# Moving the transposed activations hT by 64 bytes in SBUF

## The chip, the core and the metric

The kernel runs on one core of a Trainium2 chip. The metric is the device time of one execution in microseconds (us); lower is better. Before the change it is 2646.88 us, the median of three runs (2641.51 to 2647.48).

## What is computed

A decoder trunk of two layers over 256 tokens of width 2048, in float32. Layer 0 mixes with retention (8 heads), layer 1 with block-sparse attention (16 heads; with 256 tokens and blocks of 256 it is causal attention with a relative-position bias). Each mixer is followed by a gated MLP with a causal depthwise convolution.

```python
for i in range(DEPTH):                       # DEPTH = 2
    hn = rms_norm(h, mix_norm[i])
    h = h + (retention_mixer(hn, ret_w_in[0], ret_gn[0], ret_w_out[0]) if i == 0
             else moba_mixer(hn, moba_w_qkv[0], moba_w_out[0], rel_bias))
    h = h + conv_ffn(rms_norm(h, ffn_norm[i]), ffn_w_up[i], ffn_conv_w[i],
                     ffn_conv_b[i], ffn_w_down[i])
return rms_norm(h, final_norm)
```

The weight matrices are 2048 x 12288 and 4096 x 2048 (retention), 2048 x 6144 and 2048 x 2048 (attention), and per MLP 2048 x 11264 and 5632 x 2048. They are read once, some 480 MB, and with 256 tokens every one of them is multiplied by a small activation matrix.

## The kernel before

**Products.** A float32 value is split into a high part in fp32r and the rest, also in fp32r; a product is the sum of high by high, high by low and low by high. The activations are kept transposed, 128 channels per partition chunk: `hT` is a tile of 128 partitions x 16 chunks x 512 elements, where the first 256 elements of a chunk are the high parts of the 256 tokens and the last 256 the low parts. `yT` (32 chunks, retention output), `oT` (16 chunks, attention output) and `actT` (44 chunks, MLP inner activations) have the same layout.

**The weight stream.** Weights come as units of 1 MB by DMA (`issue_dma`, three `raw` buffers). `issue_split` cuts a unit into two halves of 128 x 1024 and makes of each a high part `wh` (ScalarE, L125) and a low part `wl` (VectorE, L126), three buffers each, two half units ahead of the products (`LOOKAHEAD = 2`). `run` walks through all half units in the order in which `emit` queued them; small tasks (scores, transposes, norms) are put between half units by `after`.

**Two kinds of panels.** In a TensorE product one operand is loaded into the array (LDWEIGHTS, the stationary operand, always 128 columns here) and the other streams past it (the moving operand).

- `panel_a` (L175 to L177): the activations are stationary, 128 tokens of one chunk, and 512 columns of weights move. Three products per chunk and token half. It is used with `hT` for gate and value of retention and for the values of attention, with `yT`, `oT` and `actT` for the three kinds of output projections.
- `panel_b` (L225 and L227): 128 columns of the weights are stationary. With `wh`, all 512 elements of an `hT` chunk move (L225); with `wl`, the first 256 (L227). The two alternate. It is used for q and k and for the whole up projection of both MLPs, always with `hT`.

The small products of the heads go through `mm3` (L239 to L241); `to_T` transposes by TensorE (L249) and writes `hT` and `yT` (L252 on ScalarE, L255 on VectorE).

**Where the tiles lie.** Pools are laid out in the order in which they are opened, and tiles within the pool `cst` one behind the other, each rounded up to 32 bytes per partition. The built program has these start addresses (bytes within a partition):

| tile | start | modulo 128 | modulo 256 |
|---|---|---|---|
| ident | 16512 | 0 | 128 |
| h | 17024 | 0 | 128 |
| hT | 33408 | 0 | 128 |
| wh, three buffers | 96576, 100672, 104768 | 64 | 64 |
| wl, three buffers | 108864, 112960, 117056 | 64 | 64 |
| actT, oT | 123456 | 64 | 64 |
| yT | 133696 | 64 | 64 |
| ph, sg, vh of retention | 199232, 200768, 220736 | 64 | 64 |
| qT, kT of retention | 211008, 215104 | 64 | 64 |
| vh, pTh of attention | 164416, 213056 and four more | 64 | 64 |

The chunks of hT, yT, oT and actT are 2048 bytes apart, and the parts of a chunk or of a weight half that a product takes begin at multiples of 512 bytes, so that every operand of a product has the residue of its tile.

Of the kernel before, what the change touches and what calls it, by code (L numbers as in the profile page):

```python
# [10 lines left out]
F32 = mybir.dt.float32  # L11
# [6 lines left out]
P = 128  # L18
D = 2048
S = 256  # L20
# [35 lines left out]
def build(tc, a, out):  # L56
    nc = tc.nc
    ctx = ExitStack()
    cst = ctx.enter_context(tc.tile_pool(name="cst", bufs=1))
# [12 lines left out]

    ident = cst.tile([P, P], F32, name="ident")
    h = cst.tile([P, 2, D], F32, name="h")
    hT = cst.tile([P, KC, 2 * S], F32R, name="hT")
    gains = cst.tile([P, 96], F32, name="gains")
    cw = [cst.tile([P, 4, 2 * NFB], F32, name=f"cw{i}") for i in range(2)]
    ones = cst.tile([P, P], F32, name="ones")
# [2 lines left out]
    rB = cst.tile([P, S], F32, name="rB")  # L81
    rBq = cst.tile([P, S], F32, name="rBq")

# [1 line left out]
    units = []  # L85

    def unit_a(w, k0, n0):
# [5 lines left out]
    halves = []  # L93
# [6 lines left out]
    def issue_dma(u):  # L100
        src, n = units[u]
        raws[u] = wraw.tile([P, 2048], F32, name="raw")
        dst = raws[u].rearrange("p (c n) -> p c n", n=n)
        if u == 0:
            # the first halves of x and of two panels come first: the products start on them
            m = dst.shape[1] // 2
            load_x(0)
            nc.sync.dma_start(dst[:, :m], src[:, :m])
            load_x(1)
            nc.sync.dma_start(dst[:, m:], src[:, m:])  # L110
        else:
            nc.sync.dma_start(dst, src)
        if u == 1:
            load_x(2)
            load_x(3)
# [43 lines left out]
                halves.append(lambda mm=mm, i=len(halves): mm(*parts.pop(i)))  # L159

    def finish(done, acc):
        # tasks that done() puts off are counted from the next half unit
        state["mm"] += 1
        done(acc)
        state["mm"] -= 1

    def panel_a(w, nk, n0, xT, done, before=None, split_last=0):
        """Tokens by 512 channels, x stationary. With split_last, the last half units run for the first token half
        and only then for the second, and done(acc, t) is called for each."""
        box, late, items = {}, [], []  # L170

        def mm_t(t, k, c, wh, wl):
            acc, xt = box["acc"][t], xT[0]
            xh, xl = xt[:, k, t * P : (t + 1) * P], xt[:, k, S + t * P : S + (t + 1) * P]
            pe.matmul(acc, lhsT=xh, rhs=wh[:, c, :], start=(k == 0), stop=False)  # L175
            pe.matmul(acc, lhsT=xh, rhs=wl[:, c, :], start=False, stop=False)  # L176
            pe.matmul(acc, lhsT=xl, rhs=wh[:, c, :], start=False, stop=(k == nk - 1))  # L177

        for k0 in range(0, nk, 2):
            def mm(wh, wl, k0=k0):  # L180
                if k0 == 0:
                    if before is not None:
                        before()
                    if split_last:
                        box["acc"] = [pacc.tile([P, 2, 512], F32, name="acc")[:, 0, :] for _ in range(2)]
                    else:
                        acc = pacc.tile([P, 2, 512], F32, name="acc")
                        box["acc"] = [acc[:, 0, :], acc[:, 1, :]]
                        box["tile"] = acc
                if k0 >= nk - 2 * split_last:  # L190
                    late.append((k0, wh, wl))
                    for c in range(2):
                        mm_t(0, k0 + c, c, wh, wl)
                else:
                    for c in range(2):
                        for t in range(2):
                            mm_t(t, k0 + c, c, wh, wl)
                if k0 == nk - 2:
                    if not split_last:
                        return finish(done, box["tile"])  # L200
                    done(box["acc"][0], 0)
                    for kl, wh, wl in late:
                        for c in range(2):
                            mm_t(1, kl + c, c, wh, wl)
                    done(box["acc"][1], 1)
            if k0 % 4 == 0:
                items.append((unit_a(w, k0, n0), [mm]))
            else:
                items[-1][1].append(mm)
        return items  # L210

    def panel_b(w, n0, xT, done, before=None):
        """256 channels by tokens, w stationary; the sum of a column and of the one S further is the value."""
        box, items = {}, []
        for k0 in range(0, KC, 4):
            def mm(wh, wl, k0=k0):
                if k0 == 0:
                    if before is not None:
                        before()
                    box["acc"] = pacc.tile([P, 2, 512], F32, name="acc")  # L220
                acc, xt = box["acc"], xT[0]
                for c in range(4):
                    k = k0 + c
                    for b in range(2):
                        pe.matmul(acc[:, b, :], lhsT=wh[:, c, b * P : (b + 1) * P], rhs=xt[:, k, :],  # L225
                                  start=(k == 0), stop=False)
                        pe.matmul(acc[:, b, S:], lhsT=wl[:, c, b * P : (b + 1) * P], rhs=xt[:, k, :S],  # L227
                                  start=False, stop=(k == KC - 1))
                if k0 == KC - 4:
                    finish(done, box["acc"])  # L230
            if k0 % 8 == 0:
                items.append((unit_b(w, k0, n0), [mm]))
            else:
                items[-1][1].append(mm)
        return items

# [1 line left out]
    def mm3(dst, lh, ll, rh, rl, start, stop):  # L238
        pe.matmul(dst, lhsT=lh, rhs=rh, start=start, stop=False)  # L239
        pe.matmul(dst, lhsT=lh, rhs=rl, start=False, stop=False)  # L240
        pe.matmul(dst, lhsT=ll, rhs=rh, start=False, stop=stop)  # L241

    def to_T(dstT, k0, src, g0, n):
        """dstT[:, k0 + i] <- (hi | lo) of the transposed src chunks, scaled by gains[:, g0 + i]."""
        for c0 in range(0, n, 2):
            pt = paux.tile([P, 2, S], F32, name="aux")
            for i in range(2):
                for t in range(2):
                    pe.transpose(pt[:, i, t * P : (t + 1) * P], src(t, c0 + i), ident)  # L249
            for i in range(2):  # L250
                g = gains[:, g0 + c0 + i : g0 + c0 + i + 1]
                act.activation(dstT[:, k0 + c0 + i, :S], pt[:, i, :], AF.Copy, scale=g)  # L252
            for i in range(2):
                g = gains[:, g0 + c0 + i : g0 + c0 + i + 1]
                dve.scalar_tensor_tensor(dstT[:, k0 + c0 + i, S:], pt[:, i, :], g,  # L255
                                         dstT[:, k0 + c0 + i, :S].bitcast(F32), op0=ALU.mult, op1=ALU.subtract)
# [40 lines left out]
        return done  # L297

    def out_proj(w, nk, xT, g0, use_r, tail=None):
        """h += xT.T @ w; then hT <- gained h, transposed, and its rms factor by use_r."""  # L300
        for j in range(4):
            def done(acc, j=j):
                residual(j)(acc)
                if g0 is not None:
                    after(2 if j < 3 else 1, lambda: h_T(j, g0))
                    if j == 3:
                        after(2, lambda: use_r())
            emit(panel_a(w, nk, j * 512, xT, done))

# [1 line left out]
    dma0 = nc.scalar.dma_start  # L311
    nc.sync.dma_start(ident, a["c_ident"])
    grow = scr.tile([P, P], F32, name="grow", tag="diag")
# [39 lines left out]
        dma0(rows["oh"], a["c_onehot"])  # L353

    def bias_table():
        """The bias by distance, one copy per query, so that a row step one short of a copy skews them."""
        pt = paux.tile([P, 512], F32, name="aux")
        pe.matmul(pt[:, : 3 * P], lhsT=rows["rb"], rhs=rows["oh"], start=True, stop=True)
        tbl = ret["p1"].tile([P, 3 * P], F32, name="tbl", tag="m1")
        dve.tensor_copy(tbl[:, :S], pt[:, :S])  # L360
        dve.memset(tbl[:, S:], NEG)
        dma0(tblD, tbl[:AH])
# [11 lines left out]
        pools[name] = es  # L374
        return es

# [1 line left out]
    w_in = a["ret_w_in"][0]  # L378
    ret = {}
    yT = [None]  # L380
# [69 lines left out]
        ret["p", hd] = (ph, pl)  # L450

    def ret_pv(hd):
        """y = silu(g) * (o - mean) * rstd per token and head, in sg's place."""
        ph, pl = ret.pop(("p", hd))
        vh, vl = ret["v"]
        sg = ret["sg"]
# [65 lines left out]
    for hd in range(RH):  # L522
        ret_head(hd)

# [1 line left out]
    ffn = {}  # L526
    actT = [None]

# [48 lines left out]
        return done  # L577

    def last_half(acc, t):
        """The last panel of one token half, and then that half's norm and store."""  # L580
        hs = h[:, t, 3 * 512 :]
        dve.tensor_tensor(hs, acc, hs, op=ALU.add)
        square_t(3, t)
# [46 lines left out]
            ffn_open()  # L630
        return f

# [1 line left out]
    mob = {}  # L634
    oT = [None]
    w_qkv = a["moba_w_qkv"][0]
# [108 lines left out]
                    after(2 + n, lambda n=n: mob_pv(g, n))  # L745
            emit(panel_a(w_qkv, KC, 2 * D + g * 512, xT_h, v_done))

# [1 line left out]
    out_proj(a["ret_w_out"][0], 2 * KC, yT, 32, lambda: make_rB(use_rB))  # L749
    ffn_layer(0, ffn_begin("ret"), 16, lambda: make_rB(use_mob), False)  # L750
    moba()
# [28 lines left out]
```

## Time and profile before

| | |
|---|---|
| median of three runs | 2646.88 us (2641.51 to 2647.48) |
| span of the profiled execution | 2645.3 us |
| TensorE busy with products (PE) | 2628.2 us, 99% |
| TensorE loading stationary operands (PEld) | 2231.6 us, 84% |
| VectorE (DVE) | 1667.2 us, 63% |
| ScalarE (ACT) | 1299.8 us, 49% |

The span runs from the first to the last instruction of the profiled execution; the median lies 1.6 us above it. In the profile a product's row has its start and a modelled end: products overlap, one of 512 columns is shown with 0.39 us though the next one starts some 0.23 us later. The time that a product costs is therefore the distance from its start to the next start, and where many are alike, a stretch of time divided by the number of products that start in it.

### The profile page before, as it was taken

To read this page: it belongs to the slowest core of one execution; us is meant where nothing else is said; L and a number is where in the kernel's file an instruction comes from. 1 tells how busy PE (TensorE), PEld (TensorE's weight loads), DVE (VectorE), ACT (ScalarE), POOL (GpSimd) and SP (SyncE) were. 2 spreads that over 40 slices of the span, in tenths; PEclk is the share of its full clock that TensorE was granted. 3 is DMA by queue.
4 is the path that set the end of the run, shared out by engine and by line. 5 is a ranking of instruction groups with operands and counts; after the bars stand their busy time and mean duration, and the time that the engine had idled before them with its cause. 6 is when DMAs were issued, how large, how long until landed. Compare 5 with 4: busy or idle time off the path is not lost.

```text
span 2645.3 us, 33493 instructions
## 1 busy us (share of the span) xinstructions
PE 2628.2 (99%) x13492; PEld 2231.6 (84%) x13492; DVE 1667.2 (63%) x2090; ACT 1299.8 (49%) x1658; POOL 10.2 (0%) x24
## 2 busy tenths in 40 slices
PE   8999999999999999999999999999999999999998
PEld 7888888888888888888888888888888888888887
DVE  5666565555557777777545566665677777775454
ACT  5444444444445555555444454454555555554443
POOL 0000000000000000000000000000000000000000
PEclk9999999999999999999999999999999999999999
DMA  7655555555555555555555655555555555556554
GB/s 235 225 181 175 177 170 190 176 175 184 191 182 191 186 182 190 189 181 187 191 191 191 200 190 174 175 185 173 178 191 187 181 189 190 181 186 207 192 194 155
DMA packets 372550, 493.85 MB, mean 187 GB/s; under 512 B 7932, under 2 KB 258860, under 8 KB 372140
## 3 DMA queue, kind: packets, MB, share of 16 engines
q1 hardware_dynamic: 366048, 482.44, 54.9%
q10 hardware_dynamic: 6348, 9.29, 1.1%
q8 instruction: 105, 1.72, 0.3%
q14 instruction: 49, 0.40, 0.0%
HBM read 489.57 MB, written 5.27 MB: 187 GB/s over the span
## 4 chain that ended last, share of the span: by engine, by line
PE 98%; DMA 1%; ACT 0%; issue 0%; DVE 0%; ACTq 0%; POOL 0%; POOLq 0%; DVEq 0%
PE acc L225 33%; PE acc L227 17%; PE acc L175 15%; PE acc L177 15%; PE acc L176 15%; PE aux L249 1%; PE aux L240 1%; PE aux L241 1%; PE aux L239 1%; DMA raw<-in_ret_w_in_dram 1%; DMA crow<-in_ffn_conv_b_dram 0%; PE aux L704 0%; ACT hT L252 0%; ACT junk L263 0%; PE aux L288 0%
## 5 line engine op out<-in xcount | busy, mean ns | idle before, releaser
L126 DVE TENSOR_TENSOR wl<-raw,wh 128x1024 fp32r<-128x1024 f32 x912 | 1116.7, 1225 | 904.3 <-ACT wh L125 901.0
L125 ACT ACTIVATE wh<-raw 128x1024 fp32r<-128x1024 f32 x912 | 967.0, 1060 | 1238.8 <-PE acc L177 601.7
L225 PE MATMUL acc<-hT,wh 128*128 128x512 f32 x3840 | 1361.9, 396 | 2.0 <-ACT wh L125 1.0
L227 PE MATMUL acc<-hT,wl 128*128 128x256 f32 x3840 | 1083.5, 282 | 0.0
L225 PEld LDWEIGHTS acc<-hT,wh 128*128 128x128 f32 x3840 | 722.5, 188 | 175.7 <-DVE hT L255 1.5
L227 PEld LDWEIGHTS acc<-hT,wl 128*128 128x128 f32 x3840 | 722.0, 188 | 1.0
L175 PE MATMUL acc<-wh,actT 128*128 128x512 f32 x704 | 274.1, 390 | 0.0
L177 PE MATMUL acc<-wh,actT 128*128 128x512 f32 x704 | 273.9, 389 | 0.0
L176 PE MATMUL acc<-wl,actT 128*128 128x512 f32 x704 | 273.9, 389 | 0.0
L175 PE MATMUL acc<-wh,hT 128*128 128x512 f32 x640 | 254.8, 398 | 0.0
L176 PE MATMUL acc<-wl,hT 128*128 128x512 f32 x640 | 253.1, 395 | 0.0
L177 PE MATMUL acc<-wh,hT 128*128 128x512 f32 x640 | 253.0, 395 | 0.0
L177 PEld LDWEIGHTS acc<-wh,actT 128*128 128x128 f32 x704 | 132.1, 188 | 27.6
L175 PEld LDWEIGHTS acc<-wh,actT 128*128 128x128 f32 x704 | 132.1, 188 | 27.6 <-DVE h L295 0.2
L176 PEld LDWEIGHTS acc<-wl,actT 128*128 128x128 f32 x704 | 132.2, 188 | 27.2
L555 DVE SCALAR_TENSOR_TENSOR t<-u,cw,t 128x256 f32<-128x256 f32 x352 | 146.7, 479 | 0.0
L177 PEld LDWEIGHTS acc<-wh,hT 128*128 128x128 f32 x640 | 120.3, 188 | 29.0
L175 PEld LDWEIGHTS acc<-wh,hT 128*128 128x128 f32 x640 | 120.3, 188 | 27.5
L176 PEld LDWEIGHTS acc<-wl,hT 128*128 128x128 f32 x640 | 120.4, 188 | 27.1
L175 PE MATMUL acc<-wh,yT 128*128 128x512 f32 x256 | 100.0, 390 | 0.0
L177 PE MATMUL acc<-wh,yT 128*128 128x512 f32 x256 | 99.6, 389 | 0.0
L176 PE MATMUL acc<-wl,yT 128*128 128x512 f32 x256 | 99.6, 389 | 0.0
(136 smaller groups left out, 1463.3 us busy)
## 6 DMA issues: line engine op xcount, KB each, us to landing
raw<-in_ffn_w_up_dram SPq DMA_DIRECT2D x176, 1024.0 KB, 5.0
raw<-in_ret_w_in_dram SPq DMA_DIRECT2D x95, 1024.0 KB, 5.0
raw<-in_ffn_w_down_dram SPq DMA_DIRECT2D x88, 1024.0 KB, 5.0
raw<-in_moba_w_qkv_dram SPq DMA_DIRECT2D x48, 1024.0 KB, 5.1
raw<-in_ret_w_out_dram SPq DMA_DIRECT2D x32, 1024.0 KB, 5.0
raw<-in_moba_w_out_dram SPq DMA_DIRECT2D x16, 1024.0 KB, 5.0
skewD<-tblD ACTq DMA_DIRECT2D x1, 3072.0 KB
h<-in_x_dram SPq DMA_DIRECT2D x4, 512.0 KB, 7.8
```

Of the source, the lines that this page charges most:

```text
L125: act.activation(wh, r, AF.Copy)
L126: dve.tensor_tensor(wl, r, wh.bitcast(F32), op=ALU.subtract)
L175: pe.matmul(acc, lhsT=xh, rhs=wh[:, c, :], start=(k == 0), stop=False)
L176: pe.matmul(acc, lhsT=xh, rhs=wl[:, c, :], start=False, stop=False)
L177: pe.matmul(acc, lhsT=xl, rhs=wh[:, c, :], start=False, stop=(k == nk - 1))
L225: pe.matmul(acc[:, b, :], lhsT=wh[:, c, b * P : (b + 1) * P], rhs=xt[:, k, :], start=(k == 0), stop=False)
L227: pe.matmul(acc[:, b, S:], lhsT=wl[:, c, b * P : (b + 1) * P], rhs=xt[:, k, :S], start=False, stop=(k == KC - 1))
L239: pe.matmul(dst, lhsT=lh, rhs=rh, start=start, stop=False)
L240: pe.matmul(dst, lhsT=lh, rhs=rl, start=False, stop=False)
L241: pe.matmul(dst, lhsT=ll, rhs=rh, start=False, stop=stop)
L249: pe.transpose(pt[:, i, t * P : (t + 1) * P], src(t, c0 + i), ident)
L555: dve.scalar_tensor_tensor(t[:, i, :], u[:, i, tap : tap + S], c[:, tap, b : b + 1], t[:, i, :], op0=ALU.mult, op1=ALU.add)
```

## The change

Two tiles of 16 float32 (64 bytes per partition) are allocated in the pool `cst`, one ahead of `hT` and one behind it. Nothing reads or writes them. In the built program hT begins at 33472, which is 64 modulo 128 and 192 modulo 256. All tiles behind it lie 128 bytes higher than before: their residue modulo 128 is the old one, and those that had 64 modulo 256 (weights, yT, oT, actT and the tiles of the heads) have 192. ident and h stay where they were. No instruction is added, removed or moved: the five engines' instructions are the same, in the same order, with the same shapes.

```diff
     ident = cst.tile([P, P], F32, name="ident")
     h = cst.tile([P, 2, D], F32, name="h")
+
+    cst.tile([P, 16], F32, name="gap0")
     hT = cst.tile([P, KC, 2 * S], F32R, name="hT")
+    cst.tile([P, 16], F32, name="gap1")
     gains = cst.tile([P, 96], F32, name="gains")
```

The rest of the diff takes out comments and docstrings. The line numbers of everything behind this place are 3 higher after the change (L225 is L228, L175 is L178).

## Rows read from the trace of the kernel before

**Rows 1.** The profile's page: busy time and share of the span of each engine; the span in 40 slices (busy tenths of PE, the granted clock of TensorE in tenths, the DMA engines' busy tenths); the chain that ended last, by engine.

```profile
PE 2628.2 (99%) x13492; PEld 2231.6 (84%) x13492; DVE 1667.2 (63%) x2090; ACT 1299.8 (49%) x1658; POOL 10.2 (0%) x24
PE   8999999999999999999999999999999999999998
PEclk9999999999999999999999999999999999999999
DMA  7655555555555555555555655555555555556554
PE 98%; DMA 1%; ACT 0%; issue 0%; DVE 0%; ACTq 0%; POOL 0%; POOLq 0%; DVEq 0%
```

**Rows 2.** The waits of PE: who it waited for, us in total, times, the longest.

```profile
PE aux L249 <- DMA h<-in_x_dram: 3.5, 2, 3.0
PE aux L322 <- DMA ident<-in_c_ident_dram: 2.9, 1, 2.9
PE acc L225 <- ACT wh L125: 1.0, 1, 1.0
PE acc L225 <- DVE hT L255: 0.8, 1, 0.8
PE aux L288 <- DVE diag L287: 0.5, 1, 0.5
```

**Rows 3.** The groups of instructions, shapes kept apart: line, engine, operation, output and inputs, shapes, count; busy us, mean ns of one; idle before.

```profile
L225 PE MATMUL acc<-hT,wh 128*128 128x512 f32 x3840 | 1361.9, 396 | 2.0 <-ACT wh L125 1.0 <-DVE hT L255 0.8
L227 PE MATMUL acc<-hT,wl 128*128 128x256 f32 x3840 | 1083.5, 282 | 0.0
...
L177 PE MATMUL acc<-wh,actT 128*128 128x512 f32 x704 | 273.9, 389 | 0.0
...
L177 PE MATMUL acc<-wh,hT 128*128 128x512 f32 x640 | 253.0, 395 | 0.0
...
L177 PE MATMUL acc<-wh,yT 128*128 128x512 f32 x256 | 99.6, 389 | 0.0
...
L177 PE MATMUL acc<-wh,oT 128*128 128x512 f32 x128 | 49.9, 390 | 0.0
```

**Rows 4.** Busy time of each engine in four stretches, with the number of instructions (x). The first is the up projection of the first MLP (L225 and L227 alone on PE), the second its down projection (L175 to L177 with actT), the third the last retention value panel (L175 to L177 with hT), the fourth the retention output projection (L175 to L177 with yT). Columns: stretch, its us, busy us and count of PE, PEld, DVE, ACT, POOL, granted clock, DMA share, GB/s.

```profile
800.00:1200.00 400.00, 400.00 (x2266) 348.40 (x2266) 296.18 (x388) 221.62 (x282) 0.00 (x0) 1.00 0.56 187
1268.00:1332.00 64.00, 64.00 (x284) 52.97 (x283) 33.78 (x34) 28.67 (x32) 0.00 (x0) 1.00 0.59 198
556.00:588.00 32.00, 32.00 (x139) 25.76 (x137) 14.44 (x15) 13.35 (x14) 0.00 (x0) 1.00 0.55 190
690.00:728.00 38.00, 38.00 (x169) 31.45 (x169) 18.36 (x16) 16.11 (x19) 0.00 (x0) 1.00 0.57 188
```

**Rows 5.** Timeline of PE around 165 us, where the products of one retention head (L239 to L241, operands vh, vl, ph, pl) stand between panels with hT. Columns: start, us shown, engine, line, operation, output and inputs, shapes.

```profile
158.24 0.40 PE L175 MATMUL acc<-wh,hT 128*128 128x512 f32 x1
...
159.64 0.40 PE L225 MATMUL acc<-hT,wh 128*128 128x512 f32 x1
...
165.23 0.40 PE L239 MATMUL aux<-vh,ph 128*128 128x512 f32 x1
165.46 0.39 PE L240 MATMUL aux<-vl,ph 128*128 128x512 f32 x1
...
167.05 0.39 PE L241 MATMUL aux<-vh,pl 128*128 128x512 f32 x1
167.28 0.40 PE L225 MATMUL acc<-hT,wh 128*128 128x512 f32 x1
```

**Rows 6.** Timeline of PE at two places where products of 256 moving columns follow each other, none with hT: retention scores (six of 256 columns from 196.25 on, then of 128) and attention values (three from 1588.43 on, then of 128).

```profile
196.25 0.28 PE L239 MATMUL aux<-qT,kT 128*128 128x256 f32 x1
...
196.96 0.22 PE L239 MATMUL aux<-qT,kT 128*128 128x128 f32 x1
...
1588.43 0.28 PE L239 MATMUL aux<-pTh,vh 128*128 128x256 f32 x1
1588.54 0.28 PE L240 MATMUL aux<-pTl,vh 128*128 128x256 f32 x1
1588.66 0.28 PE L241 MATMUL aux<-pTh,vl 128*128 128x256 f32 x1
1588.78 0.22 PE L239 MATMUL aux<-pTh,vh 128*128 128x128 f32 x1
```

**Rows 7.** Timeline of products and loads in a q or k panel of the attention layer (L225 and L227): when a load starts beside the product that runs.

```profile
1703.17 0.28 PE L227 MATMUL acc<-hT,wl 128*128 128x256 f32 x1
1703.18 0.19 PEld L225 LDWEIGHTS acc<-hT,wh 128*128 128x128 f32 x1
1703.29 0.39 PE L225 MATMUL acc<-hT,wh 128*128 128x512 f32 x1
1703.30 0.19 PEld L227 LDWEIGHTS acc<-hT,wl 128*128 128x128 f32 x1
```

**Rows 8.** Timeline of PE: eight transposes of sg and eight of h, each with ident as the other operand, and the product behind them.

```profile
602.12 1.04 PE L249 MATMUL aux<-ident,sg 128*128 128x128 f32 x8
602.91 0.47 PE L175 MATMUL acc<-wh,yT 128*128 128x512 f32 x1
...
641.12 1.04 PE L249 MATMUL aux<-ident,h 128*128 128x128 f32 x8
641.91 0.48 PE L175 MATMUL acc<-wh,yT 128*128 128x512 f32 x1
```

## The prediction

> **What bounds the kernel now.** I read the page first: is there one engine that sets the time? PE is busy 99% of the span in every slice but the first and the last, the chain that ended last is PE for 98%, and its granted clock stands at full speed, 2.4 GHz, throughout [rows 1]. All its waits together are under 9 us, most of them at the start for data [rows 2]. So nothing but the cost of the products themselves can move this kernel, and every nanosecond taken off each product shows in full, as long as no other engine becomes late.
>
> Next I asked what a product costs, and whether equal products cost the same. They don't. L177 has the same code, shapes and kinds of operands with hT, yT, oT and actT, yet with hT one is shown with 395 ns, with yT and actT with 389 and with oT with 390 [rows 3]. Shown durations are modelled, so I counted starts instead. A stretch of W us counts the products that start in it, and the one that still runs at its beginning, so I add one shown duration, 0.39 us, to W. With actT: 64.39 us by 284 is 226.7 ns. With yT: 38.39 by 169 is 227.2. With hT: 32.39 by 139 is 233.0. In the up projection, where L225 (512 columns) and L227 (256) alternate, 1133 pairs in 400.3 us are 353.3 ns a pair [rows 4].
>
> Is it the stage or the operand? The timeline tells: in one place, within 9 us, six products with hT take 1.40 us (158.24 to 159.64), 233 ns each, and then the nine of a head's vh and ph take 2.05 us (165.23 to 167.28), 228 ns each, with panels of hT around them on both sides [rows 5]. DVE and ACT do the same splitting of weights all the while. So the surplus of 6.3 ns (233.0 less 226.7) goes with hT. Of what the program gives hT and not the others, only its address is left: oT has hT's shape and strides. hT lies at 0 modulo 128; every operand of the cheap products, both of them, lies at 64.
>
> The surplus doesn't grow with the columns. If a product of 512 costs 233.0 in a pair too, one of 256 costs 120.3, where half of a cheap product would be 113.4: again 6 to 7 ns. What is the same for both is the load: each product has the next stationary operand loaded beside it, beginning 10 ns after its start [rows 7]. My reading is that the two reads of SBUF, the moving one and the load, get into each other's way where their tiles differ by 64 modulo 128. That reading is an inference; the rows show the surplus and the operand, not the collision.
>
> **The change, part by part.** It adds no instruction and takes none away, and the two gaps are never touched, so there is no new work, no new wait and nothing that needs a cover. 128 bytes more of SBUF cost no time. What it does is to give hT the residue of its partners. Four terms, by the profiled execution:
>
> 1. panel_a with hT, 3 x 640 products [rows 3]. The partner in kind is L175 to L177 with actT, identical in everything but the address: 233.0 to 226.7, 6.3 ns x 1920 = 12.1 us. This term has a direct model in the trace.
> 2. L225, 3840 products of 512 columns [rows 3]. Here hT moves and the weights are loaded. Products of 512 with all residues at 64 cost 226.7 to 228 in every place that I found [rows 4, 5]; whether hT moves or stands it now costs the same 233. I take 6.3 ns x 3840 = 24.2 us.
> 3. L227, 3840 products of 256 columns. Lower end of what they can cost: half of 226.7, 113.4, a gain of 6.9 ns. Upper end: no gain, 120.3. Between them stand the products of 256 without hT: six scores take 0.71 us, 118.3 each, and three value products 0.35, 116.7 each [rows 6]. They are free of hT and still above 113.4; I take it that the load sets the pace there, since it starts with the product before it and the next product starts some 0.11 us later [rows 7], and a product of 256 is hardly longer than that. The same holds for L227, within which a load must fit. I take 117.0, nearest to these rows: 3.3 ns x 3840 = 12.7 us, with 0 and 26.5 as ends.
> 4. The transposes that read or fill hT, and the writes by L252 and L255: ACT and DVE are off the path, and eight transposes take 0.79 us whether their source lies at 0 (h) or at 64 (sg) modulo 128 [rows 8]. Zero.
>
> Sum: 12.1 + 24.2 + 12.7 = 49.0 us. The span goes from 2645.3 to 2596.3, and with the 1.6 us that the median lies above the span the forecast is **2597.9 us**, 1.9% faster. With term 3 at its ends the time is 2610.6 or 2584.1.
>
> Does something else become late? A unit of 1 MB feeds 16 pairs of panel_b; at 343.7 ns a pair (226.7 + 117.0) that is 5.50 us. With actT a unit feeds 24 products of 226.7 ns, 5.44 us, and there PE is busy 64.00 of 64.00 us, at a DMA share of 0.59 [rows 4]. So the stream is already taken at this pace without a wait. DVE is busy 296 of 400 us in the up projection [rows 4]; at the new pace this is 74% x 353.3 / 343.7 = 76%. Neither becomes the bound.
>
> The Trainium skill speaks against the change. "SBUF — State Buffer", section "SBUF: two separate sides", says that on the engine side only a port pair that VectorE and GpSimd share causes contention and that PE never waits on anyone; "TensorE: Matmul & The Clock Gate", section "Step-by-step: what each phase is for", says that TensorE has two independent SBUF read ports and that a load doesn't take read bandwidth from the running product. By these pages an address that suits the bytes can't matter, the gain would be 0 and the time 2646.9. They don't account for the two costs that the rows show for one and the same product. The outcome would be that of the first rival below.
>
> **The rivals.**
>
> *No change, 2646.9 us.* The surplus may hang on something else in hT's place: it is the one large operand that lies below the weights, at 33 to 66 thousand bytes, where all cheap ones lie above 96 thousand. After the change it still does. For it: the trace has no cheap wide product from that region. Transposes, which have ident at 0 and sg at 64, show no surplus against h at 0 [rows 8]; if residues that differ always collided, one might expect some. But these have 128 columns of another kind and tell little on products that stream 512. Chance 0.10.
>
> *Only one side is cured.* Stationary hT has a model in the trace, moving hT with alternating widths has none. If only term 1 comes: 2646.9 - 12.1 = 2634.8. If only terms 2 and 3: 2646.9 - 36.9 = 2610.0. Chance 0.08 together, spread between these.
>
> *Slower, about 2667.* One mechanism: what counts is not the residue modulo 128 but whether the address has the 128-byte bit set. hT has it now (128 modulo 256), and all partners of the cheap products don't (64). The second gap pushes every one of them to 192, so that they all have it, and hT, at 192, has it still. Then every product costs the surplus: L175 to L177 with yT, actT and oT are 3 x (256 + 704 + 128) = 3264 [rows 3] at 6.3 ns, 20.6 us, 2667.5 us. It decides as soon as that bit counts at all. For it: in the rows before the two properties go together in every wide product, so they can't be told apart. Against it: relative positions explain why both ways of using hT cost alike without asking for a bit that is bad in itself, and ident and h, which have the bit, show nothing [rows 8]. Chance 0.05.
>
> *A new bound* (DMA or DVE late at the new pace) would give back part of the gain; the stage with actT speaks against it. Chance 0.01.
>
> **How the numbers follow.** The forecast case, both sides cured with term 3 anywhere between its ends, gets 0.76 and spans 2584 to 2611. A measurement of this kernel can tell some 0.3% (8 us) from no change, that is, faster means under 2639. The forecast, the one-sided cure and the small rest are faster: 0.84. No change: 0.11, with a trifle for effects of a few microseconds. Slower: 0.05. For the range, the forecast case alone isn't enough for 8 in 10; with the one-sided cases up to 2635 it is 0.84. Below I allow 4 us under 2584, since the runs shown spread by 5 below their median. Range 2580 to 2636.
>
> **What would show it.** In the profile after, L177 with hT (L180 then) should be shown with about 389 ns like actT, not 395, and L225 (L228) with about 390, not 396 [rows 3]. In the stretch of the up projection the pairs should come every 343 to 347 ns; a pair of 353 with the products of stationary hT at 227 would mean the one-sided cure, and waits of PE for `wh` or `wl`, beyond the microsecond of now [rows 2], a new bound. Products with actT must stay at 227: if they go to 233, the slower rival holds. If hT's products stay at 233 and actT's at 227, the residue modulo 128 was not the cause, and the place of hT or something that I haven't seen is. If L225 falls to 227 and L227 stays at 120, term 3 was the wrong part.

## The result: 0.85% faster, half of the forecast

The changed kernel takes 2621.85 us (median of 4 runs, 2618.52 to 2628.19) against 2647.14 us for the kernel before (4 runs, 2641.51 to 2647.48): a ratio of 0.9915, 95% interval 0.9892 to 0.9938. The forecast was 2597.9 us, a gain of 49.0; what came is 25.3. The profiled execution of the changed kernel is its slowest, 2628.19 us with a span of 2626.1.

Busy times of the engines on the page of the changed kernel; compare [rows 1]:

```profile
PE 2608.1 (99%) x13492; PEld 2225.7 (85%) x13492; DVE 1666.0 (63%) x2090; ACT 1300.3 (50%) x1658; POOL 10.2 (0%) x24
```

PE is still the bound, and its granted clock stands at 1.00 in every stretch shown below, as before. Its groups of instructions, lines 3 higher than before; compare [rows 3]:

```profile
L228 PE MATMUL acc<-hT,wh 128*128 128x512 f32 x3840 | 1353.1, 397 | 3.4 <-DVE hT L258 1.8 <-ACT wh L128 1.5
L230 PE MATMUL acc<-hT,wl 128*128 128x256 f32 x3840 | 1078.1, 281 | 0.0
...
L180 PE MATMUL acc<-wh,actT 128*128 128x512 f32 x704 | 274.0, 389 | 0.0
...
L180 PE MATMUL acc<-wh,hT 128*128 128x512 f32 x640 | 249.4, 390 | 0.0
```

The products with hT stationary went from 395 ns shown to 390, those with actT stayed at 389. But L228, which should have gone from 396 to 390, is shown with 397. Shown durations are modelled, so starts are counted again. The stretches, with the columns of [rows 4]: the up projection of the first MLP, the last retention value panel, the up projection of the second MLP.

```profile
800.00:1200.00 400.00, 400.00 (x2265) 346.90 (x2265) 297.03 (x391) 222.06 (x283) 0.00 (x0) 1.00 0.57 186
...
556.00:588.00 32.00, 32.00 (x143) 26.50 (x142) 15.95 (x16) 15.04 (x16) 0.00 (x0) 1.00 0.57 192
1950.00:2350.00 400.00, 400.00 (x2309) 352.69 (x2308) 301.48 (x397) 227.26 (x290) 0.00 (x0) 1.00 0.58 190
```

Counted as in the prediction, the products with hT stationary now take 32.39 us by 143, 226.5 ns each. The first up projection runs at 800.6 by 2265, 353.5 ns a pair, as before. The second one, the same code on the same tiles, runs at 800.6 by 2309, 346.7. In the kernel before, the second up projection had the pace of the first:

```profile
1950.00:2350.00 400.00, 400.00 (x2266) 348.28 (x2265) 297.20 (x392) 222.33 (x284) 0.00 (x0) 1.00 0.57 187
```

By these stretches the gain of the profiled execution is 6.5 ns x 1920 = 12.5 us from panel_a and (353.4 - 346.7) x 1408 pairs = 9.4 us from one of two up projections, 21.9 together. The span fell by 19.2; the sum over every product, further below, shows where the rest went. Two paces in one execution of one code call for an explanation that residues alone don't give.

The timeline of PE shows the two paces directly. Columns as in [rows 5]; first six pairs in the first up projection, then six in the second, each with the start of what follows.

```profile
899.33 0.28 PE L230 MATMUL acc<-hT,wl 128*128 128x256 f32 x1
899.45 0.40 PE L228 MATMUL acc<-hT,wh 128*128 128x512 f32 x1
...
901.45 0.28 PE L230 MATMUL acc<-hT,wl 128*128 128x256 f32 x1
```

```profile
1999.26 0.28 PE L230 MATMUL acc<-hT,wl 128*128 128x256 f32 x1
1999.37 0.39 PE L228 MATMUL acc<-hT,wh 128*128 128x512 f32 x1
1999.60 0.28 PE L230 MATMUL acc<-hT,wl 128*128 128x256 f32 x1
...
2001.34 0.28 PE L230 MATMUL acc<-hT,wl 128*128 128x256 f32 x1
```

901.45 - 899.33 is 2.12 us, 353 ns a pair; 2001.34 - 1999.26 is 2.08, 347. Nothing waits in either. The starts in the trace also tell the two products of a pair apart, from each start to the next. Before, between 800 and 1200 us, L225 (512 columns) took 233.5 ns and L227 (256) 119.9. After, in the same window of the slow up projection, they take 236.4 and 116.9; in the fast one, between 1950 and 2350 us, 230.0 and 116.7. So the product of 256 columns became cheaper at both paces, and the one of 512 became dearer at the slow pace.

### The profile page after: what moved, and what is told of

Same layout as the page of the kernel before. It is cut to its first block, busy times and chain, and to the rows that moved or that the text cites. A ratio compares the mean times of both kernels' runs of the same rounds, so it can differ in the third digit from the quotient of the medians.

```text
span 2626.1 us, 33493 instructions
## 1 busy us (share of the span) xinstructions
PE 2608.1 (99%) x13492; PEld 2225.7 (85%) x13492; DVE 1666.0 (63%) x2090; ACT 1300.3 (50%) x1658; POOL 10.2 (0%) x24
## 4 chain that ended last, share of the span: by engine, by line
PE 98%; DMA 1%; ACT 0%; issue 0%; DVE 0%; ACTq 0%; POOL 0%; POOLq 0%; DVEq 0%
PE acc L228 33%; PE acc L230 17%; PE acc L178 15%; PE acc L179 15%; PE acc L180 15%; PE aux L252 1%; PE aux L243 1%; PE aux L244 1%; PE aux L242 1%; DMA raw<-in_ret_w_in_dram 1%; DMA crow<-in_ffn_conv_b_dram 0%; PE aux L707 0%; ACT hT L255 0%; ACT junk L266 0%; PE aux L291 0%
## 5 line engine op out<-in xcount | busy, mean ns | idle before, releaser
L228 PE MATMUL acc<-hT,wh 128*128 128x512 f32 x3840 | 1353.1, 397 | 3.4 <-DVE hT L258 1.8
L228 PEld LDWEIGHTS acc<-hT,wh 128*128 128x128 f32 x3840 | 721.0, 188 | 173.8 <-DVE hT L258 2.5
L178 PE MATMUL acc<-wh,actT 128*128 128x512 f32 x704 | 274.1, 390 | 0.0
L178 PE MATMUL acc<-wh,hT 128*128 128x512 f32 x640 | 251.3, 393 | 0.0
L180 PE MATMUL acc<-wh,hT 128*128 128x512 f32 x640 | 249.4, 390 | 0.0
L178 PEld LDWEIGHTS acc<-wh,actT 128*128 128x128 f32 x704 | 132.2, 188 | 27.6 <-DVE h L298 0.2
L178 PEld LDWEIGHTS acc<-wh,hT 128*128 128x128 f32 x640 | 120.2, 188 | 24.0
L178 PE MATMUL acc<-wh,yT 128*128 128x512 f32 x256 | 99.9, 390 | 0.0
```

## Experiments

Three theories stood against each other. **A**: a product's cost follows from how the addresses of its two operands lie to each other. **B**: it follows from each operand's own residue (64 good, 0 bad). **C**: alternating products fall into a rhythm, one of several steady paces, when a stretch is entered, and stay in it. A2, in the later expectations, is A with the difference of the two addresses (moving less stationary) taken modulo 256.

### The products alone (e1_residues_alone)

The trunk is replaced by stretches of products on two tiles X (stationary) and W (moving), both beginning at 0 modulo 128 (and at 128 modulo 256). The core of the edit, where `widths` is (512,), (512, 256), (512, 512, 256, 256) or (256,), and `s` and `m` are the offsets in bytes:

```diff
+    def stretch(name, widths, s, m, n, c=P):
...
+        for i in range(n):
+            w = widths[i % len(widths)]
+            pe.matmul(acc[:c, :w], lhsT=stat(X, i % 16, s)[:, :c], rhs=mov(W, i, m, w), start=(i == 0), stop=(i == n - 1))
```

> The products by themselves: nothing of the trunk is computed. Random data lie in two tiles that begin at 0 modulo 128; the stationary operand is taken 0 or 64 bytes in, the moving one 0, 32, 64 or 96 bytes in. Stretches of 48 to 52 products: wide (512 moving columns), pair (512 and 256 in turn), duo (512, 512, 256, 256), half (256), few (512, with 64 stationary columns in place of 128), both (stationary at 64), bothpair (pair, stationary at 64). Theory A, relative residue: wide0 and both64 226.7 ns a product, wide64 and both0 233. If the load takes 32 cycles of 2.4 GHz from the running product, as 226.7 = (512 + 32) / 2.4 suggests, then pair0 346.7 ns a pair = (768 + 64) / 2.4, half0 120 = (256 + 32) / 2.4, few0 220 = (512 + 16) / 2.4. Theory B, absolute residue of 64: both64 226.7, wide0 233. Theory C, the rhythm: pair0 goes into one of several rhythms by how it was entered, 346.7 or 353.3 ns a pair, and stays in it, whatever the residues. What 32 and 96 give is open: under A with lines of 64 bytes 233 like 64, with lines of 16 bytes 226.7.

The timeline of PE, merged by stretch: start, us, engine, line, operation, operands (numbers left out of names), shapes, count. In the order of the program the first wide row has W at 0, the second at 32 bytes, the third at 64; half is at 0, then at 64; both has X at 64 and W at 0, then both at 64.

```profile
24.87 11.04 PE L86 MATMUL wide<-W,X 128*128 128x512 f32 x48
35.75 8.63 PE L86 MATMUL pair<-W,X 128*128 128x512 f32 x48
44.22 8.52 PE L86 MATMUL duo<-W,X 128*128 128x512 f32 x48
52.58 11.36 PE L86 MATMUL wide<-W,X 128*128 128x512 f32 x48
63.77 8.50 PE L86 MATMUL pair<-W,X 128*128 128x512 f32 x48
72.11 8.49 PE L86 MATMUL duo<-W,X 128*128 128x512 f32 x48
80.44 11.16 PE L86 MATMUL wide<-W,X 128*128 128x512 f32 x48
91.44 8.63 PE L86 MATMUL pair<-W,X 128*128 128x512 f32 x48
...
136.21 22.16 PE L86 MATMUL few<-W,X 128*64 128x512 f32 x96
158.21 5.92 PE L86 MATMUL half<-W,X 128*128 128x256 f32 x48
163.96 11.37 PE L86 MATMUL both<-W,X 128*128 128x512 f32 x48
175.17 8.64 PE L86 MATMUL bothpair<-W,X 128*128 128x512 f32 x48
183.64 5.82 PE L86 MATMUL half<-W,X 128*128 128x256 f32 x48
189.30 11.11 PE L86 MATMUL both<-W,X 128*128 128x512 f32 x48
200.24 8.63 PE L86 MATMUL bothpair<-W,X 128*128 128x512 f32 x48
```

From one start to the next, by the count: wide at 0 takes 10.88 us by 48, 226.7 ns; wide at 32, 11.19, 233.1; both with W at 0, 11.21, 233.5; both with both at 64, 10.94, 227.9. With X and W at 0 the product is cheap, so B falls. A holds in that operands that agree are cheap, and no engine but PE works during these stretches, so VectorE, ScalarE and DMA have no part in it. But wide at 64 takes 11.00 by 48, 229.2, where A, modulo 128, expected 233: X ahead of W by 64 bytes and W ahead of X by 64 don't cost the same.

My price for a load fails: few, with half the stationary columns (48 products with W at 0, then 48 at 64), takes 22.00 by 96, 229 ns, not 220. The pair at 0 takes 8.47 by 24, 353 ns, at 32 8.34, 347.5: here the pair is slow where the wide product is fast. And for rows of 256 columns alone agreement isn't best: half at 0 is 5.75 by 48, 119.8, but at 64 it is 5.66, 117.9.

### Every difference (e5_all_differences)

The same program with W 0 to 240 bytes in, in steps of 16, in three rounds, and then pairs entered in eight ways:

```diff
+    for rep in range(3):
+        for m in range(0, 256, 16):
+            last = stretch(f"wide{chr(97 + m // 16)}", (512,), 0, m, 44 + 2 * rep)
+            last = stretch(f"pair{chr(97 + m // 16)}", (512, 256), 0, m, 44 + 2 * rep)
+    for m in (0, 32, 64, 192):
+        for pre in range(1, 9):
+            stretch("enter", (128,), 0, 0, pre)
+            last = stretch(f"in{chr(97 + m // 16)}", (512, 256), 0, m, 46)
```

> The products by themselves again, nothing of the trunk is computed. Moving operand 0 to 240 bytes further in than the stationary one's residue, in steps of 16 (letter a is 0, c 32, e 64, i 128, m 192), wide (512 columns) and pair (512 and 256 in turn), three times each, and then pairs at 0, 32, 64 and 192 entered behind one to eight products of 128 columns. Theory A in its first form (agree or differ modulo 128): a and i alike, e and m alike. Theory A2, the difference moving minus stationary modulo 256: e and m differ (wide 229 and 233), and each letter has its own cost. Theory C: the pairs at one difference take more than one pace by how they are entered (353.3 and 346.7 ns a pair at 0). If one difference gives one pace for all eight entries, C falls for that difference.

Timeline of PE as above; the first rows are wide products at 0 (a), 64 (e), 128 (i) and, from the third round, 64 again, each with the start of what follows. The rows from 943.21 on are pairs at 0 and at 32 (inc).

```profile
25.71 10.14 PE L86 MATMUL widea<-W,X 128*128 128x512 f32 x44
35.69 7.92 PE L86 MATMUL paira<-W,X 128*128 128x512 f32 x44
...
97.16 10.25 PE L86 MATMUL widee<-W,X 128*128 128x512 f32 x44
107.24 7.84 PE L86 MATMUL paire<-W,X 128*128 128x512 f32 x44
...
168.76 10.43 PE L86 MATMUL widei<-W,X 128*128 128x512 f32 x44
179.03 7.88 PE L86 MATMUL pairi<-W,X 128*128 128x512 f32 x44
...
690.96 11.36 PE L86 MATMUL widee<-W,X 128*128 128x512 f32 x48
702.16 8.54 PE L86 MATMUL paire<-W,X 128*128 128x512 f32 x48
...
943.21 8.33 PE L86 MATMUL ina<-W,X 128*128 128x512 f32 x46
951.38 0.56 PE L86 MATMUL enter<-W,X 128*128 128x128 f32 x4
951.78 8.20 PE L86 MATMUL ina<-W,X 128*128 128x512 f32 x46
959.81 0.67 PE L86 MATMUL enter<-W,X 128*128 128x128 f32 x5
...
1011.48 8.19 PE L86 MATMUL inc<-W,X 128*128 128x512 f32 x46
1019.51 0.56 PE L86 MATMUL enter<-W,X 128*128 128x128 f32 x4
```

Wide products in the first round: 9.98 us by 44, 226.8 ns at 0; 10.08, 229.1 at 64; 10.27, 233.4 at 128; 233.2 at 192. At 0, 128 and 192 the other rounds agree. At 64 the second round gives 229 again and the third 233.3 (11.20 by 48): wide products too can have two paces, and one price for each letter, as A2 had it, fails there. 0 and 128 differ in every round, so it isn't the residue modulo 128 that counts. Among the sixteen, 0 alone gives 227, in all three rounds. A period of 256 fits the kernel before: there actT lies 26880 bytes above the first buffer of wh, 105 times 256, and its products cost 226.7. Differences of 256 and more weren't tried here.

Pairs, and here C holds: at 0 the 23 pairs took 8.17 us behind three products (943.21 to 951.38) and 8.03 behind four (951.78 to 959.81), same operands, same code; of eight entries five took the slow pace and three the fast one. Each entry was tried once. At 32 (c) all eight took 8.03. The fast pace, without the first products, is 346.7 ns a pair, the slow one some 353.5. At 64 seven of eight entries took 353 and one 348.9; at 192 all eight took 353.3. The rule of one pace for each difference thus falls at 0 and at 64, and stands at 32 and at 192 as far as these entries go.

### Moving the tiles of the whole kernel (e2, e3, e4)

Each is the kernel before with one gap, at another place or of another size:

```diff
# e2_all_at_0
     hT = cst.tile([P, KC, 2 * S], F32R, name="hT")
+    cst.tile([P, 16], F32, name="gap1")
# e3_hT_64_rest_0
+    cst.tile([P, 16], F32, name="gap0")
     hT = cst.tile([P, KC, 2 * S], F32R, name="hT")
# e4_hT_0_rest_moved_128
     hT = cst.tile([P, KC, 2 * S], F32R, name="hT")
+    cst.tile([P, 32], F32, name="gap1")
```

> Gap of 64 bytes behind hT alone: hT stays at 0 modulo 128 and the weights, yT, oT and actT move from 64 to 0. Theory A (what counts is whether the two operands agree): panel_a with hT 227 ns as in the changed kernel, with actT 227, time 2618 to 2628. Theory B (64 is good in itself): panel_a with hT and with actT 233, time 2647 + 20 = 2667. Theory C on the pairs: 346.7 or 353.3 in long stretches, each switch of one up projection 9.4 us.

> Gap of 64 bytes ahead of hT alone: hT at 64 modulo 128, the weights, yT, oT and actT at 0. Theory A: they differ as in the kernel before, panel_a with hT 233, with actT (0 with 0) 227, time 2641 to 2648. Theory B (hT at 64 is what helps): panel_a with hT 227 and a time of 2618 to 2628, or with actT 233 if 0 is bad for any operand.

> Gap of 128 bytes behind hT alone: residues modulo 128 as in the kernel before, and the rest at 192 modulo 256 as in the changed one. If the residue modulo 128 is all that counts: panel_a with hT 233, time 2641 to 2648. If the move of the rest by 128 took part in the gain: 227 with hT, 2618 to 2628.

Stretches as in [rows 4]: first up projection, last retention value panel, second up projection; first e2, then e3, then e4.

```profile
800.00:1200.00 400.00, 400.00 (x2310) 352.74 (x2309) 301.46 (x398) 227.01 (x290) 0.00 (x0) 1.00 0.59 190
...
556.00:588.00 32.00, 32.00 (x143) 26.48 (x142) 17.45 (x18) 13.99 (x15) 0.00 (x0) 1.00 0.58 192
1950.00:2350.00 400.00, 400.00 (x2310) 352.75 (x2309) 301.44 (x399) 227.09 (x289) 0.00 (x0) 1.00 0.58 190
```

```profile
556.00:588.00 32.00, 32.00 (x140) 25.84 (x140) 14.56 (x14) 13.23 (x15) 0.00 (x0) 1.00 0.58 192
1950.00:2350.00 400.00, 400.00 (x2295) 350.32 (x2294) 299.37 (x396) 224.71 (x286) 0.00 (x0) 1.00 0.58 189
```

```profile
556.00:588.00 32.00, 32.00 (x141) 26.30 (x140) 15.18 (x15) 15.04 (x16) 0.00 (x0) 1.00 0.61 197
```

| kernel | hT, others (modulo 256) | us | ratio, 95% interval | hT stationary, ns |
|---|---|---|---|---|
| e2 | 128, 128 | 2615.76 | 0.989 (0.9869 to 0.9911) | 226.5 |
| e3 | 192, 128 | 2636.83 | 0.9977 (0.9961 to 0.9994) | 231.4 |
| e4 | 128, 192 | 2640.74 | 0.9982 (0.9971 to 0.9993) | 229.7 |

e2 leaves hT where it was and moves its partners to it: the whole gain and more, in all four runs (2615.16 to 2616.47), and both up projections at the fast pace, 346.6. B falls here too. e3 gives hT the address of the change but not the partners: its 231.4 is the 233.0 of before within the count (140 products for 139 in the same 32 us), so no gain in panel_a; its small gain is the rhythm, the second up projection at 800.6 by 2295, 348.8. e4 is the difference of 64 for panel_a (weights less hT), which e5 prices at 229 in two rounds of three; it takes 229.7, where a rule modulo 128 wanted 233. That expectation missed. One product more or less in such a stretch is 1.6 ns, so the mean over all 1516 distances between neighbouring products of the retention panels of panel_a decides: 233.8 before, 227.4 after, 233.8 in e3 and 229.5 in e4.

### The changed kernel again (e6_after_again)

No edit.

> The changed kernel as it is, a second look, for the spread of its runs and the pace of each up projection. Theory C: each up projection (1408 pairs) runs throughout at 353.3 or at 346.7 ns a pair, so that times fall in steps of about 9.4 us: both slow 2628, one fast 2618 to 2626, both fast 2612 to 2616; panel_a with hT at 227 in every run. Rival, a steady gain: all runs within 3 us of 2622 and both up projections at one pace.

Median 2618.72 (2618.1 to 2627.5), ratio 0.9904 (0.9887 to 0.992). Of the four runs three lie at 2618 to 2619 and one, the profiled one, at 2627.5: two groups, 9 us apart, as C wants; a steady gain falls. The stretches of the profiled run:

```profile
800.00:1200.00 400.00, 400.00 (x2267) 346.76 (x2266) 296.91 (x391) 221.77 (x283) 0.00 (x0) 1.00 0.58 186
1950.00:2350.00 400.00, 400.00 (x2310) 352.69 (x2309) 301.50 (x398) 226.80 (x289) 0.00 (x0) 1.00 0.59 190
```

Again the first up projection is slow and the second fast. The expectation put such a run at 2618 to 2626 and had 2628 for both slow; with one fast it took 2627.5. That the 2618 runs have both fast is worked out (2627.5 - 9.4 = 2618.1); they have no profile. The same goes for the 2618.52 and 2618.56 of the first comparison; its 2625.14 fits neither group and stays unexplained.

### Choosing the difference for each kind of panel (e7, e8, e9)

e7 is the kernel before with hT 32 above all weights:

```diff
     hT = cst.tile([P, KC, 2 * S], F32R, name="hT")
+    cst.tile([P, 8], F32, name="gap1")
```

> A gap of 32 bytes behind hT alone, so that hT lies at 128 and the weights, yT, oT and actT at 96 modulo 256: the moving hT of panel_b is 32 above the weights, the moving weights of panel_a are 224 above hT. Theory A2 (each kind of product by the difference moving minus stationary modulo 256, as in the stretches of e5): pairs 346.7 ns throughout (letter c), panel_a with hT 233.4 (letter o), with actT 227. Time 3840 x 6.6 = 25 us under before, 2620, and close together, since c knew one pace. Rival (only agreement helps): pairs 353, time 2645.

e8 has difference 0 for panel_a and 32 for panel_b; e9 has the same tiles with `o = 8` for both kinds. The lines of the edit that set the difference; the others, the same in e8 and e9, are the gaps and the small tiles that the expectation names.

```diff
-        wh = whi.tile([P, 1024], F32R, name="wh")
-        wl = wlo.tile([P, 1024], F32R, name="wl")
+        o = 8 if units[u][1] == 512 else 0
+        wh = whi.tile([P, 1024 + 64], F32R, name="wh")[:, o : o + 1024]
+        wl = wlo.tile([P, 1024 + 64], F32R, name="wl")[:, o : o + 1024]
```

> The halves of weights for panel_b begin 32 bytes lower in their tiles than those for panel_a (tiles 256 bytes wider; to make room rBq moves into the attention layer's pool, junk shares a buffer with diag, and six small tiles share theirs in pairs). hT, yT, oT, actT and the panel_a weights at 160, the panel_b weights at 128 modulo 256. Theory A2: pairs 346.7 ns in every stage, panel_a with hT 227: 25 + 12 = 37 us under before, 2608, in every run. Theory C for all (a rhythm that any start may set): times spread over 2608 to 2628.

> As e8, but the panel_b weights too begin at 160 like hT: the same tiles in the same places, difference 0 for both kinds. Panel_a with hT 227; pairs at 346.7 or 353.3 by stage, as at difference 0 in e5, so 2615 to 2628. If this is as fast as e8, the difference of 32 has no part in it and the moved small tiles have.

The last value panel of e7, then the three stretches of e8, then the two up projections of e9:

```profile
556.00:588.00 32.00, 32.00 (x139) 25.77 (x138) 14.04 (x12) 13.33 (x14) 0.00 (x0) 1.00 0.54 178
```

```profile
800.00:1200.00 400.00, 400.00 (x2310) 354.61 (x2310) 301.50 (x397) 226.66 (x288) 0.00 (x0) 1.00 0.58 190
...
556.00:588.00 32.00, 32.00 (x143) 26.51 (x142) 19.30 (x23) 13.33 (x14) 0.69 (x1) 1.00 0.57 192
1950.00:2350.00 400.00, 400.00 (x2310) 354.61 (x2309) 301.48 (x398) 226.90 (x289) 0.00 (x0) 1.00 0.58 190
```

```profile
800.00:1200.00 400.00, 400.00 (x2310) 352.69 (x2309) 301.67 (x399) 227.60 (x289) 0.00 (x0) 1.00 0.58 190
...
1950.00:2350.00 400.00, 400.00 (x2267) 346.99 (x2266) 297.96 (x393) 224.03 (x285) 0.00 (x0) 1.00 0.57 186
```

| kernel | us (range) | ratio, 95% interval |
|---|---|---|
| e7 | 2624.00 (2622.49 to 2624.09) | 0.9934 (0.9921 to 0.9946) |
| e8 | 2612.38 (2610.68 to 2612.55) | 0.9890 (0.9877 to 0.9903) |
| e9 | 2616.74 (2616.08 to 2626.49) | 0.9919 (0.9903 to 0.9935) |

e7 pays 233 in panel_a (32.39 by 139) and gains in the pairs alone, whose up projections run at 346.6 as in e8 (not shown); its five runs lie within 1.6 us, 2 to 4 above the 2620 expected. e8 has 346.6 in both up projections and 226.5 in panel_a; its four runs lie within 2 us, 3 to 5 us above the 2608 expected. e9, the same tiles without the split, has two groups again, four runs at 2616 to 2617 and two at 2626, with the slow pace this time in the second up projection. So the moved small tiles don't make e8 steady; that the difference of 32 does rests on the eight entries of e5, the five runs of e7 and these four, for e2, at difference 0, had four runs as close together. e8 has the shortest times here, but measured against the kernel before in its own comparison it is level with e2: a ratio of 0.989 each.

## Why the forecast was twice too large

**What bounds the kernel** was right: PE is busy 99% of the span before and after, no new bound came, and DVE and DMA keep the faster pace.

The terms can be checked one by one. All traces have the same 13492 products in the same order, so the distance from each start to the next can be compared product by product with the kernel before. Sums in us, rounded, from the profiled executions:

| products | forecast | changed kernel | e2 | e8 |
|---|---|---|---|---|
| panel_a with hT (term 1) | -12.1 | -11.3 | -11.6 | -11.5 |
| 512 columns in panel_b (term 2) | -24.2 | +2.1 | -8.4 | -19.1 |
| 256 columns in panel_b (term 3) | -12.7 | -11.1 | -12.5 | -5.5 |
| all others | 0 | +1.2 | +1.0 | -0.4 |
| sum | -49.0 | -19.2 | -31.4 | -36.6 |

**Term 1** (panel_a with hT, 12.1 us) was right: 233.0 to 226.5 in the stretch, 11.3 us over all panels. It rested on rows of the same kind of product with other addresses.

**Term 2** (512 columns in panel_b, 24.2 us) is the step that failed. The forecast borrowed 226.7 ns from L175 to L177 for L225, because products of 512 columns cost 226.7 to 228 in every place found. Those places all had products of equal width in a row. In alternation with 256 columns the product takes 230.0 ns at the fast pace and 236.4 at the slow one, where it took 233.5 before. In place of a gain of 24.2 us the profiled execution lost 2.1, which is 26 of the 30 us that are missing from its span. Even e2, with both up projections at the fast pace, gains only 8.4 here.

**Term 3** (256 columns in panel_b, 12.7 us) came: 116.7 and 116.9 ns at the two paces against the forecast's 117.0, 11.1 us in all. The reason given for it, that the load sets the pace, wasn't tested, and rows of 256 columns alone at difference 0 cost 119.8 in e1, so this may be luck.

Behind term 2 stands a premise: that one pair of residues gives one price. In e1 and e5 the cheapest pair at any of the sixteen differences takes about 346 ns, never the 343.7 of the forecast, and at difference 0 the pair has two paces, some 346.7 and 353.3, the second as dear as before the change. The working allowed for a gain of 0 in term 3, but not for a pair that stays at its old price as a whole. The pairs of all panels could give at most (353.3 - 346.7) x 3840 = 25.3 us; e8 comes near with 19.1 + 5.5 = 24.6. The stated range held the measured 2621.85 us only because it had been widened for the one-sided cure.

**The reading of the cause** was half right. Shown: the surplus depends on the difference between the stationary and the moving operand's addresses, with all other engines idle, and moving the partners helps as moving hT does. Wrong was the modulus: differences of 0 and 128 cost 226.8 and 233.4 in e5; a period of 256 fits the rows of this case. The Trainium skill, "SBUF — State Buffer", section "SBUF: two separate sides", has PE never waiting on anyone. That leaves no room for the 226.8 and 233.4 ns of e5, one product at two offsets with no other engine at work; the measurement decides. That the two reads collide in SBUF is still an inference, and why 32 suits pairs and 0 wide products stays open.

**Which rhythm a stretch takes** is open too. In e5 the pace at difference 0 changed with the number of products ahead, tried once for each number, and at 32 it didn't. What in a panel's start selects it in the kernel wasn't tried. Part of the measured gain hangs on it, for the kernel before has two paces as well: pooled over all comparisons, its fastest run, 2632.85 us, lies 14.8 us above the fastest of the changed kernel, 2618.10, and its slowest, 2648.20, lies 20.0 above the slowest, 2628.19. The 11 us of panel_a are gained at either pace; how much more shows depends on the paces that the compared runs took.

**The rivals.** No change falls: the gain is there. Slower, by the 128-byte bit, falls: yT, oT and actT stayed at 389 to 393 shown with all of them at 192 modulo 256, the products with actT take 226.9 ns from start to start in both traces, and e2 has all wide operands at 128 without a loss. The one-sided cure came nearest: where hT is stationary, the surplus went wholly; where it moves, the pairs of the profiled execution gave 11.1 - 2.1 = 9.0 of 36.9 us, a quarter.

## What to carry to other kernels

When equal products cost differently, compare the addresses of their two operands, the difference modulo 256 bytes, before their stages; two gaps of 64 bytes were worth 0.85% here, and one gap (e2) or an offset for each kind of panel (e8) 1.1%. A price may be carried over only to products in the same sequence of widths: what was 226.7 ns in a row of equals was 228 to 236 in alternation. If the time of a kernel falls into groups a few microseconds apart, count starts per stage in the profile: in these traces a stage of 1408 pairs kept one of two paces throughout.

## What the hardware showed unexpectedly

Products that wait for nothing had rhythms here. Pairs of 512 and 256 columns at difference 0 repeat at 346.7 or at 353.3 ns, for 500 us at a stretch, and four products of 128 columns ahead of them in place of three switched the pace (8.03 against 8.17 us for 23 pairs). At the fast pace every pair is alike, 230 and 117 ns; at the slow one the starts repeat every three pairs, around 1000 us in the changed kernel with 236, 233 and 241 ns for 512 columns and 113, 117 and 120 for 256. The kernel before has two paces too: at its difference of 64 the up projections ran at 353 in its profile, and at 348.8 in one of e3, which has the same difference. Halving the stationary columns saved nothing: 229 ns, a mean over offsets 0 and 64, where 128 columns cost 226.8 and 229.1.
